# A two-layer diffusion trunk on one core: layer norm's mean held to an upper place, output projection begun with attention's half, adaLN units released by twos

## The chip, the cores and the metric

The kernel runs on one core of one Trainium2 chip. The metric is the device time of one execution in microseconds (us); the time of the kernel before is the median of three runs. Smaller is better.

## The reference

One inference step of a two-layer trunk over T = 384 tokens (128 context tokens, 256 latent tokens), width D = 2048, all in float32. Cut to what this case touches (layer 0, the even one):

```python
sh, sc, gt = split(silu(c) @ w_mod + b_mod, 3)            # adaLN, for each layer
h = rms_norm(x, g) * (1 + sc) + sh
ga, gb, gate_a, q, k, v, gate_b = split(h @ w_in)
a = depthwise_conv(ga * sigmoid(gb), conv_w) + conv_b     # 31 taps
a = silu(layer_norm(a, ln_g, ln_b)) * silu(gate_a)        # 1024 channels: conv's half
b = attention(q, k, v) * silu(gate_b)                     # 8 heads of 128: attention's half
x = x + gt * (concatenate([a, b]) @ w_out)
```

Layer 1 follows with another attention and a short convolution, then a final rms norm.

## The kernel before

Activations lie feature by token: `x["T"]` and `mix` are 16 chunks k of 128 features by 384 tokens. In `mix` of layer 0 chunks 0 to 7 are the conv's half, chunks 8 to 15 attention's half. Every large product is done with float32 operands split in two: `split` makes a high part on ScalarE (ACT) and the rest on VectorE (DVE), `hhi`/`hlo` for the activations and `whi`/`wlo` for a weight tile `raw`, and TensorE (PE) does three products, (hi, hhi), (hi, hlo), (lo, hhi).

A feature pass is `proj_feat`: 256 output features (two PSUM accumulators, a `pair()` out of five banks `acc`), 16 chunks, in two units of 8 chunks, `feat_unit`; a unit is two halves `hf` of four chunks, each with a weight tile of its own. A tile is used by 24 products of 128 x 384, a pass by 96. `whi` and `wlo` have three buffers each (`NHI`, `NLO`), so that a tile's casts wait until PE has left the tile three before it; `raw` has six.

Layer 0 runs feature passes for conv (`w0[0..7]`), then gate_a (`w0[8..11]`), gate_b (`w0[12..15]`), then the output projection `out_proj` (eight passes `fb`, 768 products) and on to layer 1. The conv's 31 taps run on DVE beside the passes, and attention's small products (`s_ps`, `pT_ps`, `o_ps`) stand on PE between the products of the passes. After the first gate_b pass the code calls `ln_mean` (sum of the conv's chunks `lsum`, a product with ones, `mean`) and `ln_center` (subtract, squares, variance `lvar`), after the second the inverse deviation (`rsl` on PE, Newton steps on DVE, `rbl` on PE, copy `rb`) and `ln_out` (a product on DVE and a SiLU on ACT per chunk), and then `mod_rows`, adaLN columns of layer 1 as dot products on DVE (L207, tile `area`). At last L799 multiplies the conv's half into `mix`.

The order on each engine is set by the tile framework, which schedules the whole program by its own timeline and by code order as priority; `tc.add_manual_dep(a, b, NOSYNC)` only forbids it to place a before b, with no semaphore. Each engine then runs its list strictly in that order. All weight loads issue from one queue, SP's, in code order (`sync_load`).

`gemv_q` holds other adaLN columns as units: a load of 1 MB to one of three lent slots (`lent`) and four thin products (`gv`, eight instructions in a trace, as float32 operands that aren't split take two). `pump`, called after each unit of a pass, releases a unit whenever `rate` has added up to one.

Of the kernel before, what the change touches and what calls it, by code (L numbers as in the profile page):

```python
# [17 lines left out]
NOSYNC = mybir.DependencyInfo(mybir.DependencyClass.NoSync, mybir.DependencyReason.DATA)  # L18
# [4 lines left out]
T = 384  # L23
# [28 lines left out]
def trunk(ctx: ExitStack, tc: tile.TileContext, d: dict, o: dict):  # L52
# [39 lines left out]
        if order["hold"] is not None:  # L92
            tc.add_manual_dep(ins, order["hold"].name, SYNC, reason="side loads wait")

    order = {"last": None, "split": None, "hold": None}

    def sync_load(dst, src):
        ins = nc.sync.dma_start(dst, src).ins
# [4 lines left out]
    def load_w(w, k0, nk, f0, nf, raw=None):  # L103
        if raw is None:
            raw = wp.tile([P, nk, nf], F32, tag="raw", name="raw")
        sync_load(raw, w[:, k0:k0 + nk, f0:f0 + nf])
        return raw
# [14 lines left out]
    def gemv_block(w, f0, nf, stat, done):  # L122
        nk = 2048 // nf
        st = {}

        def unit(u):
            if u == 0:
                st["ps"] = ps_gv.tile([P, 512], F32, tag="gv", name="gv")
            ps = st["ps"]
            slot = ring_slot()  # L130
            if slot is not None:
                raws = [load_w(w, nk * u, nk, f0, nf, slot.rearrange("p (k f) -> p k f", f=nf))]
            else:
                raws = [load_w(w, nk * u + nk // 2 * i, nk // 2, f0, nf) for i in range(2)]
            for i in range(nk):
                g = i % 4
                k = nk * u + i
                raw = raws[i * len(raws) // nk]
                nc.tensor.matmul(ps[32 * g:32 * g + 32, :nf], lhsT=stat(k), rhs=raw[:, i % raw.shape[1], :],  # L139
                                 start=(k < 4), stop=(k >= KC - 4))  # L140
            if nk * (u + 1) == KC:
                gs = tmp.tile([P, 512], F32, tag="gs", name="gs", bufs=1)
                nc.scalar.copy(gs[:, :nf], ps[:, :nf])
                done(gs, ps)
        return [lambda u=u: unit(u) for u in range(KC // nk)]

    def mod_tile(layer, part):
        m = const.tile([P, KC, 2], F32, name=f"mod{layer}{part}")
        mods[layer, part] = m
        return m  # L150

    def mod_finish(layer, part, sl, parts):
        n = sl.stop - sl.start
        b = vec(f"mod_b{layer}")[:, 16 * part:16 * part + 16]
        gn = vec(f"norm_g{layer}")
        dst = mods[layer, part][:, sl, :]
        if parts is not None:
            nc.vector.tensor_reduce(dst, parts, AX.X, ALU.add)
        bb = b[:, sl].unsqueeze(2).broadcast_to([P, n, 2])
        nc.vector.tensor_tensor(dst, dst, bb, ALU.add)  # L160
        if part == 1:
            gg = gn[:, sl].unsqueeze(2).broadcast_to([P, n, 2])
            nc.vector.scalar_tensor_tensor(dst, dst, 1.0, gg, ALU.add, ALU.mult)

    def mod_part(layer, part, widths=(512, 512, 512, 512), f0=0):
        if (layer, part) not in mods:
            mod_tile(layer, part)

        def consume(f0, nf, gs, pc):
            n = nf // P  # L170
            for i in range(n):
                nc.tensor.transpose(pc[:, i * P:(i + 1) * P], gs[:, i * P:(i + 1) * P], ident)  # L172
            sl = slice(f0 // P, (f0 + nf) // P)
            mod_finish(layer, part, sl, pc[:, :nf].rearrange("p (k g r) -> p k r g", g=4, r=32)[:, :, 0:2, :])
        units = []
        for nf in widths:
            units += gemv_block(d[f"mod_w{layer}"][4 * part + f0 // 512], f0 % 512, nf, lambda k: cst[:, 2 * k:2 * k + 32],
                                lambda gs, ps, f0=f0, nf=nf: consume(f0, nf, gs, ps))
            f0 += nf
        return units  # L180
# [101 lines left out]
    def split(dst_hi, dst_lo, src):  # L282
        nc.scalar.copy(dst_hi, src)  # L283
        order["split"] = nc.vector.tensor_tensor(dst_lo, src, dst_hi.bitcast(F32), ALU.subtract).ins  # L284
# [28 lines left out]
    gemv_q = []  # L313
    fill_q = []

    bg = {"rate": 0.0, "due": 0.0}

    def pump():
        bg["due"] += bg["rate"]
        while bg["due"] >= 1.0 - 1e-6 and gemv_q:  # L320
            bg["due"] -= 1.0
            gemv_q.pop(0)()

    @contextmanager
    def first():
# [20 lines left out]
    def load_split(w, k0, nk, nf):  # L346
        raw = load_w(w, k0, nk, 0, nf)
        hi = wp.tile([P, nk, nf], F32R, tag="whi", name="whi", bufs=NHI)
        lo = wp.tile([P, nk, nf], F32R, tag="wlo", name="wlo", bufs=NLO)
        split(hi, lo, raw)  # L350
        return hi, lo
# [22 lines left out]
    def feat_unit(pp, w, u, n, begin, end):  # L374
        for hf in range(2):
            hi, lo = load_split(w, 8 * u + 4 * hf, 4, 256)
            for j in range(2):
                fj = slice(j * P, (j + 1) * P)
                for i in range(4):
                    k = 8 * u + 4 * hf + i  # L380
                    for m, (x, y) in enumerate(((hi, hhi), (hi, hlo), (lo, hhi))):
                        ins = nc.tensor.matmul(pp[j][:, :n], lhsT=x[:, i, fj], rhs=y[:, k, :n],  # L382
                                               start=(begin and k % 8 == 0 and m == 0),
                                               stop=(end and k % 8 == 7 and m == 2)).ins
                        order["product"] = ins
            for _ in range(FILL):
                if fill_q:
                    fill_q.pop(0)()
        pump()

    def pair():
        return [acc(f"pf{j}") for j in range(2)]
# [173 lines left out]
            return go  # L566
        return ev

    def out_proj(layer, w, mix, units, each, split_last=0, between=None):
        gate = mods[layer, 2]  # L570
        for k in (*range(8 * units[0], 8 * units[0] + 8), *range(8 * units[1], 8 * units[1] + 8)):
            split(hhi[:, k, :T], hlo[:, k, :T], mix[:, k, :])

        def ev(fb):
            def go(j, ps):
                f = 2 * fb + j
                if layer == 0:
                    s = tmp.tile([P, T], F32, tag="wk", bufs=4, name="go")
                    for g, c0, c1 in GROUPS:
                        nc.scalar.activation(s[:, c0:c1], ps[:, c0:c1], AF.Copy, scale=gate[:, f, g:g + 1])  # L580
                    nc.vector.tensor_tensor(x["T"][:, f, :], x["T"][:, f, :], s, ALU.add)
                else:
                    for g, c0, c1 in GROUPS:
                        nc.vector.scalar_tensor_tensor(x["T"][:, f, c0:c1], ps[:, c0:c1], gate[:, f, g:g + 1],
                                                       x["T"][:, f, c0:c1], ALU.mult, ALU.add)
                each(f)
            return go
        for fb in range(8 - split_last):
            proj_feat(w[fb], ev(fb), units)
        held = {fb: pair() for fb in range(8 - split_last, 8)}  # L590
        for fb, pp in held.items():
            feat_unit(pp, w[fb], units[0], T, True, False)
        if between:
            between()
        for fb, pp in held.items():
            feat_unit(pp, w[fb], units[1], T, False, True)
            for j in range(2):
                ev(fb)(j, pp[j])


    w0 = d["wf0"]
# [18 lines left out]
    for j, nf in enumerate(widths):  # L620
# [7 lines left out]
        last = j == len(widths) - 1  # L628
# [36 lines left out]
    mix = big.tile([P, KC, T], F32, tag="bigB", name="mix0")  # L665
# [47 lines left out]

    def own_slots():
        ring["slots"] = slots
    gates0 = mod_part(0, 2) + mod_part(1, 1, (512,))
    gates0[0] = lambda unit=gates0[0]: (own_slots(), unit())
    gemv_q.extend(bias_q + gates0)
# [32 lines left out]
    def ln_mean():  # L751
        av = tmp.tile([P, T], F32, tag="sacc", name="lsum", bufs=1)
        nc.vector.tensor_tensor(av, apad[:, 0, :T], apad[:, 1, :T], ALU.add)
        for c in range(2, 8):
            nc.vector.tensor_tensor(av, av, apad[:, c, :T], ALU.add)
        pm = aux("mean")
        ins = nc.tensor.matmul(pm[:, :T], lhsT=ones.broadcast_to([P, P]), rhs=av, start=True, stop=True).ins
        tc.add_manual_dep(ins, order["product"].name, NOSYNC, reason="not before its place")
        ln["m"] = tmp.tile([P, T], F32, tag="rb", name="mean", bufs=1)
        nc.scalar.activation(ln["m"], pm[:, :T], AF.Copy, scale=1.0 / CW)  # L760

# [48 lines left out]
    def ahead():  # L810
        drain(gemv_q)
        for k in range(8):
            make_h(1, k)
    out_proj(0, d["w_out0"], mix, (0, 1), each, 2, ahead)


    for k in range(8, KC):
# [6 lines left out]
    mix = big.tile([P, KC, T], F32, tag="bigB", name="mix1")  # L824
# [212 lines left out]
```

## Time and profile before

| | us |
|---|---|
| median of three runs (1300.74 to 1301.24) | 1300.79 |
| the profiled execution | 1300.42 |
| its span, first to last instruction | 1298.6 |
| PE busy in the span | 1257.6 |
| DVE busy | 884.9 |
| ACT busy | 564.6 |
| what lies outside the span (1300.42 less 1298.6) | 1.8 |

Busy times add up what an engine executed. PE is busy for 97% of the span, so that nearly the whole time is its list of products, and what can be had lies in the 41 us in which it stands still and in stretches at a lower granted clock.

### The profile page before, as it was taken

Reading aid. Unit: us, or ns where it says so; the run is one execution under the profiler, and the core shown is the slowest. Engines: PE = TensorE matmul, PEld = TensorE weight load, DVE = VectorE, ACT = ScalarE, POOL = GpSimd, SP = SyncE. Lnnn points to the kernel's source line nnn. Section 1 sums busy time; section 2 is a strip of 40 time slices with the busy share of each in tenths; the row PEclk is TensorE's granted clock in tenths of the full one; section 3 lists DMA queues with packets and bytes.
Section 4 is the critical chain, followed back from the end, with each engine's and each line's share of the span. In section 5 each row is a group of like instructions: output and inputs, shape, how many; then the busy total and the mean of one; then the engine's idle time right before and its main releaser. Section 6 shows DMA issues by size and latency. Waiting matters only on the chain.

```text
span 1298.6 us, 17795 instructions
## 1 busy us (share of the span) xinstructions
PE 1257.6 (97%) x6856; PEld 1116.1 (86%) x6856; DVE 884.9 (68%) x1507; ACT 564.6 (43%) x989; POOL 96.3 (7%) x137
## 2 busy tenths in 40 slices
PE   6999999999999999599999999999999999999997
PEld 3566676888978799499999988899999999999997
DVE  2244688998989975999976942354443599994443
ACT  3345432664465655433464632254444423343322
POOL 0211100000000000111100000000000011101110
PEclk9999999999999999799999999999999999999999
DMA  9989987787554344387743444333333578844422
GB/s 367 401 305 356 342 318 289 301 321 250 188 201 146 116 163 154 108 266 255 251 155 119 129 130 125 120 120 115 100 97 106 166 259 271 267 148 129 130 65 97
DMA packets 67620, 257.97 MB, mean 199 GB/s; under 512 B 7056, under 2 KB 11408, under 8 KB 59984
## 3 DMA queue, kind: packets, MB, share of 16 engines
q1 hardware_dynamic: 54736, 203.51, 45.4%
q0 software_dynamic: 12656, 53.23, 12.0%
q8 instruction: 53, 0.87, 0.3%
q14 instruction: 31, 0.25, 0.1%
q10 hardware_dynamic: 144, 0.10, 0.0%
HBM read 253.15 MB, written 3.67 MB: 198 GB/s over the span
## 4 chain that ended last, share of the span: by engine, by line
PE 96%; DVE 2%; DMA 1%; ACT 0%; issue 0%; SPq 0%; DVEq 0%; ACTq 0%
PE pf L382 68%; PE pt L361 10%; PE q L612 6%; PE gv L139 5%; PE s_ps L505 2%; PE o_ps L530 2%; PE pT_ps L526 1%; DMA ring<-in_mod_w 1%; PE y_ps L921 1%; PE gv L172 0%; PE qT_ps L491 0%; PE gv L676 0%; DVE mix L799 0%; DVE apad L773 0%; DVE area L207 0%
## 5 line engine op out<-in xcount | busy, mean ns | idle before, releaser
L382 PE MATMUL pf<-hhi,whi 128*128 128x384 f32 (+1 forms) x1664 | 568.9, 342 | 10.9 <-ACT hhi L283 10.6
L382 PE MATMUL pf<-hlo,whi 128*128 128x384 f32 (+1 forms) x1664 | 570.9, 343 | 5.0 <-DVE hlo L284 5.0
L382 PE MATMUL pf<-hhi,wlo 128*128 128x384 f32 (+1 forms) x1664 | 565.7, 342 | 1.2 <-DVE wlo L284 1.2
L284 DVE TENSOR_TENSOR wlo<-raw,whi 128x1024 fp32r<-128x1024 f32 x256 | 313.0, 1224 | 285.5 <-ACT whi L283 280.6
L283 ACT CAST whi<-raw 128x1024 fp32r<-128x1024 f32 x256 | 268.3, 1050 | 475.1 <-PE pf L382 267.4
L382 PEld LDWEIGHTS pf<-hhi,whi 128*128 128x128 f32 x1664 | 313.6, 189 | 31.9 <-issue 14.6
L382 PEld LDWEIGHTS pf<-hhi,wlo 128*128 128x128 f32 x1664 | 313.7, 189 | 12.2 <-issue 4.7
L382 PEld LDWEIGHTS pf<-hlo,whi 128*128 128x128 f32 x1664 | 314.1, 189 | 10.8 <-DVE hlo L284 5.5
L207 DVE CUSTOM_DVE_ANT_0 area<-area,crow 128x1024 f32<-128x1024 f32 x128 | 151.3, 1218 | 4.9 <-PE o_ps L530 4.4
L702 DVE SCALAR_TENSOR_TENSOR cv<-apad,cw,cv 128x399 f32<-128x399 f32 x240 | 138.7, 628 | 0.0
L361 PE MATMUL pt<-wlo,hhi 128*128 128x512 f32 x192 | 75.8, 395 | 0.0
L361 PE MATMUL pt<-whi,hhi 128*128 128x512 f32 x192 | 75.4, 396 | 0.0
L361 PE MATMUL pt<-whi,hlo 128*128 128x512 f32 x192 | 74.1, 395 | 0.0
L91 POOL DMA_DIRECT2D area<-in_modT x64 | 33.9, 531 | 457.6 <-DVE sm L207 223.8
L276 POOL TENSOR_TENSOR sacc<-sacc,sqf 128x384 f32<-128x384 f32 x28 | 33.5, 1196 | 176.4 <-ACT sqf L275 175.6
L361 PEld LDWEIGHTS pt<-whi,hhi 128*128 128x128 f32 x192 | 36.0, 188 | 11.0 <-ACT hhi L308 1.7
L612 PE MATMUL q<-whi,hhi 128*128 128x512 f32 x96 | 41.1, 428 | 4.4 <-ACT hhi L295 4.4
L361 PEld LDWEIGHTS pt<-whi,hlo 128*128 128x128 f32 x192 | 35.9, 188 | 10.0 <-DVE wlo L284 1.7
L139 PE MATMUL gv<-ring,cst 128*32 128x512 f32 (+1 forms) x288 | 35.6, 582 | 8.6 <-DMA ring<-in_mod_w 7.7
L361 PEld LDWEIGHTS pt<-wlo,hhi 128*128 128x128 f32 x192 | 36.1, 188 | 9.1 <-issue 0.8
L513 ACT ACTIVATE pr<-s_ps,nm 128x384 f32<-128x384 f32 (+1 forms) x48 | 24.4, 509 | 44.2 <-DVE nm L512 34.4
L612 PE MATMUL q<-wlo,hhi 128*128 128x512 f32 x96 | 40.5, 422 | 0.0
(186 smaller groups left out, 1005.9 us busy)
## 6 DMA issues: line engine op xcount, KB each, us to landing
raw<-in_wf SPq DMA_DIRECT2D x144, 512.0 KB, 4.5
ring<-in_mod_w SPq DMA_DIRECT2D x32, 1024.0 KB, 7.0
raw<-in_w_out SPq DMA_DIRECT2D x64, 512.0 KB, 4.1
area<-in_modT POOLq DMA_DIRECT2D x64, 512.0 KB, 5.2
lent<-in_mod_w SPq DMA_DIRECT2D x20, 1024.0 KB, 4.9
raw<-in_wq SPq DMA_DIRECT2D x32, 512.0 KB, 8.7
raw<-in_wt SPq DMA_DIRECT2D x24, 512.0 KB, 3.6
lent<-in_modT POOLq DMA_DIRECT2D x8, 1024.0 KB, 8.2
```

The costliest lines, as they stand in the source:

```text
L91: ins = nc.gpsimd.dma_start(dst, src).ins
L139: nc.tensor.matmul(ps[32 * g:32 * g + 32, :nf], lhsT=stat(k), rhs=raw[:, i % raw.shape[1], :], start=(k < 4), stop=(k >= KC - 4))
L207: ins = nc.vector.tensor_tensor_reduce(out=raw if g else junk, in0=raw, in1=crow[:, g, h * n:(h + 1) * n], scale=1.0, scalar=0.0, op0=ALU. ...
L276: eng.tensor_tensor(av, av, s, ALU.add)
L283: nc.scalar.copy(dst_hi, src)
L284: order["split"] = nc.vector.tensor_tensor(dst_lo, src, dst_hi.bitcast(F32), ALU.subtract).ins
L361: nc.tensor.matmul(pp[t], lhsT=x[:, k, tt], rhs=y[:, i, :], start=(k == 0 and n == 0), stop=(k == KC - 1 and n == 2))
L382: ins = nc.tensor.matmul(pp[j][:, :n], lhsT=x[:, i, fj], rhs=y[:, k, :n], start=(begin and k % 8 == 0 and m == 0), stop=(end and k % 8 == ...
L505: nc.tensor.matmul(ps, lhsT=mix[:, h0 + h, t * P:(t + 1) * P], rhs=kT[:, kv, c0:c0 + nk * P], start=True, stop=True)
L530: nc.tensor.matmul(po, lhsT=v[:, slots[j], kv * HD:(kv + 1) * HD], rhs=pT[:, j, :], start=(j == 0), stop=(j == nk - 1))
L612: nc.tensor.matmul(pq[b][t], lhsT=x[:, k, tt], rhs=y[:, 0, 512 * b:512 * b + 512], start=(k == 0 and n == 0), stop=(k == KC - 1 and n == 2))
L702: nc.vector.scalar_tensor_tensor(st["o"], apad[:, c, j:j + CVW], cw[:, c, j:j + 1], st["o"], ALU.mult, ALU.add)
```

## The change

Three edits. First, the scheduler may not place the first product of the fifth weight half after `ln_mean` (that is the first product of the third gate_b pass) before the product `mean`. Second, layer 0's output projection takes chunks 8 to 15 first, then 0 to 7, and its first two passes run by halves: both passes' attention units, then both passes' conv units, with four accumulators held. The last two passes ran by halves before, and keep their order (chunks 0 to 7 first). Third, once the lent slots belong to the adaLN units, `pump` releases two at a time.

```diff
+    bg = {"rate": 0.0, "due": 0.0, "set": 1}
     def pump():
         bg["due"] += bg["rate"]
-        while bg["due"] >= 1.0 - 1e-6 and gemv_q:
-            bg["due"] -= 1.0
-            gemv_q.pop(0)()
+        while bg["due"] >= bg["set"] - 1e-6 and gemv_q:
+            bg["due"] -= bg["set"]
+            for _ in range(bg["set"]):
+                if gemv_q:
+                    gemv_q.pop(0)()
...
             hi, lo = load_split(w, 8 * u + 4 * hf, 4, 256)
+            order["halves"] += 1
...
+                        if order["must"] and order["must"][1] == order["halves"]:
+                            tc.add_manual_dep(ins, order["must"][0].name, NOSYNC, reason="not behind this place")
+                            order["must"] = None
                         order["product"] = ins
...
+        def by_halves(fbs, units, between=None):
+            held = {fb: pair() for fb in fbs}
+            for fb, pp in held.items():
+                feat_unit(pp, w[fb], units[0], T, True, False)
+            if between:
+                between()
+            for fb, pp in held.items():
+                feat_unit(pp, w[fb], units[1], T, False, True)
+                for j in range(2):
+                    ev(fb)(j, pp[j])
+        by_halves(range(split_first), units)
+        for fb in range(split_first, 8 - split_last):
             proj_feat(w[fb], ev(fb), units)
...
+        by_halves(range(8 - split_last, 8), units[::-1], between)
...
     def own_slots():
         ring["slots"] = slots
+        bg["set"] = 2
...
+        order["must"] = (ins, order["halves"] + 5)
...
-    out_proj(0, d["w_out0"], mix, (0, 1), each, 2, ahead)
+    out_proj(0, d["w_out0"], mix, (1, 0), each, 2, 2, ahead)
```

No instruction is added or taken away but for the order; the number of products, loads and casts is the same. Three places show what the scheduler made of it (line numbers of the kernel before stand some lines lower in the changed one).

On PE, at the third gate_b pass (accumulators pf_4146 and pf_4147; pf_3858 is the second pass's). Before, the last of the last head group's products (`o_ps`) and the mean stand behind 60 of the third pass's 96 products:

```order
L382 MATMUL pf_4146<-hlo,whi 128x384
L382 MATMUL pf_4146<-hhi,wlo 128x384
L530 MATMUL o_ps<-pT,kv 128x512
L757 MATMUL mean<-lsum,ones 128x384
L382 MATMUL pf_4147<-hhi,whi 128x384
```

Now:

```order
L385 MATMUL pf_3858<-hhi,wlo 128x384
L532 MATMUL pT_ps<-ident,pr 128x128 x12
L536 MATMUL o_ps<-pT,kv 128x512 x3
L768 MATMUL mean<-lsum,ones 128x384
L385 MATMUL pf_4146<-hhi,whi 128x384
L385 MATMUL pf_4146<-hlo,whi 128x384
```

The mean stands ahead of the third pass, and the last head group's transposes and products stand right before it in one block, with no product of a pass among them. Behind it, `rsl` follows after 85 products instead of 89, and `rbl` after 123 of the 192, where it stood behind all 132 that were left.

On DVE, from the fourth gate_b pass's end into the output projection (`rb` is the inverse deviation, `sg` a SiLU of gate_b, `area` the dot products of `mod_rows`). Before:

```order
L284 TENSOR_TENSOR wlo<-raw,whi 128x1024
L565 TENSOR_TENSOR mix_1217<-mix_1217,sg 128x384 x3
L773 TENSOR_TENSOR apad<-apad,rb 128x384 x8
L565 TENSOR_TENSOR mix_1217<-mix_1217,sg 128x384
L207 ISA area,sm_4046<-area,crow 128x1024
L207 ISA sm_4046 128x1
L284 TENSOR_TENSOR hlo<-mix_1217,hhi 128x384 x3
L799 TENSOR_TENSOR mix_1217<-mix_1217,apad 128x384 x7
```

Now:

```order
L785 TENSOR_TENSOR apad<-apad,rb 128x384 x8
L207 ISA area,sm_4046<-area,crow 128x1024
L207 ISA sm_4046 128x1
L811 TENSOR_TENSOR mix_1217<-mix_1217,apad 128x384 x4
L284 TENSOR_TENSOR wlo<-raw,whi 128x1024
L811 TENSOR_TENSOR mix_1217<-mix_1217,apad 128x384
L207 ISA area,sm_4046<-area,crow 128x1024
L207 ISA sm_4046 128x1
L207 ISA area,sm_4046<-area,crow 128x1024
L207 ISA sm_4046 128x1
L811 TENSOR_TENSOR mix_1217<-mix_1217,apad 128x384 x3
L284 TENSOR_TENSOR hlo<-mix_1217,hhi 128x384 x5
```

Before, `hlo` of chunks 8 to 11 stood well ahead of these rows, and the x3 are chunks 12 to 14. Now no `hlo` stands ahead of the last L811; the x5 are, by their operands, chunks 8, 9, 0, 10, 1, and what follows is: wlo, hlo of 11, 2, 3, two L207, the SiLU's product for chunk 14, hlo of 12, 13, 4, wlo, the product for chunk 15, hlo of 5, 6, 7, wlo, two L207, hlo of 14, 15.

On SP's queue, where the adaLN units' loads begin (`lent` is 1 MB, `raw` one weight tile of 512 KB). Before:

```order
L98 DMA lent<-in_mod_w 128x2048 x2
L98 DMA raw<-in_wf 128x1024 x2
L98 DMA lent<-in_mod_w 128x2048
L98 DMA raw<-in_wf 128x1024 x2
L98 DMA lent<-in_mod_w 128x2048 x2
```

Now:

```order
L98 DMA lent<-in_mod_w 128x2048
L98 DMA raw<-in_wf 128x1024 x2
L98 DMA lent<-in_mod_w 128x2048 x2
L98 DMA raw<-in_wf 128x1024 x2
L98 DMA lent<-in_mod_w 128x2048 x2
L98 DMA raw<-in_wf 128x1024 x4
```

The loads come in pairs, with four to six weight tiles between two pairs.

## Rows read from the trace of the kernel before

**Rows 1.** PE's waits, whole run: waiter, releaser, us in total, times, longest.
```profile
PE pf L382 <- ACT hhi L283: 10.6, 1, 10.6
PE pf L382 <- DVE hlo L284: 5.0, 1, 5.0
```
**Rows 2.** Stretches: busy us of each engine (instructions), PE's granted clock, DMA share, GB/s.
```profile
core 0: us, PE busy (x) PEld busy (x) DVE busy (x) ACT busy (x) POOL busy (x), PEclk, DMA share, GB/s
...
500.00:540.00 40.00, 24.42 (x136) 23.55 (x135) 34.24 (x73) 24.41 (x44) 2.84 (x2) 0.81 0.39 128
540.00:610.00 70.00, 70.00 (x396) 70.00 (x396) 67.81 (x111) 25.36 (x40) 10.20 (x19) 0.99 0.74 243
...
680.00:745.00 65.00, 65.00 (x371) 64.78 (x370) 50.36 (x107) 37.64 (x82) 1.44 (x2) 1.00 0.39 121
```
**Rows 3.** PE in order of time: start, us, instruction, idle before and its releaser.
```profile
521.10 0.93 PE L256 MATMUL rbl<-diag,ones 128*128 128x128 f32 x6
532.65 1.01 PE L382 MATMUL pf<-hhi,whi 128*128 128x384 f32 x2 [10.62 <-ACT hhi L283]
538.61 0.69 PE L382 MATMUL pf<-hlo,whi 128*128 128x384 f32 x1 [4.96 <-DVE hlo L284]
...
541.88 0.34 PE L382 MATMUL pf<-hhi,wlo 128*128 128x384 f32 x1
```
**Rows 4.** The chain that ended last, 480 to 560 us: start, us, what.
```profile
490.98 0.44 PE pT_ps L526 x4
...
495.94 0.86 PE o_ps L530 x2
496.80 0.65 PE mean L757 x2
497.44 15.60 PE pf L382 x89
513.04 0.56 PE rsl L240 x6
```
**Rows 5.** ACT in order of time, 470 to 545 us.
```profile
486.89 1.08 ACT L527 COPY pT<-pT_ps 128x512 f32<-128x512 f32 x2 [2.69 <-PE pT_ps L526]
...
521.11 1.04 ACT L283 CAST whi<-raw 128x1024 fp32r<-128x1024 f32 x1 [2.66 <-PE pf L382]
...
525.32 4.89 ACT L774 ACTIVATE apad<-apad,vecs 128x384 f32<-128x384 f32 x8
```
**Rows 6.** DVE in order of time, 522 to 545 us.
```profile
522.18 1.23 DVE L284 TENSOR_TENSOR wlo<-raw,whi 128x1024 fp32r<-128x1024 f32 x1 [0.75 <-ACT whi L283]
...
524.73 3.83 DVE L773 TENSOR_TENSOR apad<-apad,rb 128x384 f32<-128x384 f32 x8
...
528.95 1.22 DVE L207 CUSTOM_DVE_ANT_0 area<-area,crow 128x1024 f32<-128x1024 f32 x1
...
530.09 1.49 DVE L284 TENSOR_TENSOR hlo<-mix,hhi 128x384 fp32r<-128x384 f32 x3
531.50 3.36 DVE L799 TENSOR_TENSOR mix<-mix,apad 128x384 f32<-128x384 f32 x7
```
**Rows 7.** AdaLN units on PE, in the chain of the whole run.
```profile
239.96 1.85 PE gv L139 x16
...
246.02 1.00 PE gv L139 x8
```
**Rows 8.** ACT at 250 us: a weight tile's cast that waited for its load.
```profile
250.55 1.05 ACT L283 CAST whi<-raw 128x1024 fp32r<-128x1024 f32 x1 [5.35 <-DMA raw<-in_wf]
```
**Rows 9.** PE at 45 us, after 2.20 us idle (0.76 us idle stood just before).
```profile
45.87 0.50 PE L612 MATMUL q<-whi,hhi 128*128 128x512 f32 x1 [2.20 <-ACT hhi L295]
...
47.38 0.63 PE L612 MATMUL q<-wlo,hhi 128*128 128x512 f32 x1
```
**Rows 10.** Stretches of 1 us, columns as in rows 2: the clock after two idle times.
```profile
47.00:48.00 1.00, 1.00 (x4) 0.81 (x3) 1.00 (x4) 1.00 (x4) 0.00 (x0) 0.50 1.00 416
...
50.00:51.00 1.00, 1.00 (x5) 0.84 (x4) 0.00 (x0) 0.00 (x0) 0.00 (x0) 0.89 1.01 416
...
524.00:525.00 1.00, 0.00 (x0) 0.00 (x0) 1.00 (x3) 1.00 (x4) 0.00 (x0) 0.84 0.54 70
525.00:526.00 1.00, 0.00 (x0) 0.00 (x0) 1.00 (x3) 1.00 (x3) 0.00 (x0) 0.50 0.89 336
...
541.00:542.00 1.00, 1.00 (x5) 1.00 (x5) 1.00 (x2) 0.00 (x0) 0.00 (x0) 0.62 0.00 0
```

More of the change, by code (lines that the diff above doesn't have):

```diff
@@ L93, in side_load @@
             tc.add_manual_dep(ins, order["hold"].name, SYNC, reason="side loads wait")
-    order = {"last": None, "split": None, "hold": None}
+    order = {"last": None, "split": None, "hold": None, "must": None, "halves": 0}
     def sync_load(dst, src):
@@ L314, in trunk @@
     fill_q = []
-    bg = {"rate": 0.0, "due": 0.0}
+    bg = {"rate": 0.0, "due": 0.0, "set": 1}
     def pump():
         bg["due"] += bg["rate"]
-        while bg["due"] >= 1.0 - 1e-6 and gemv_q:
-            bg["due"] -= 1.0
-            gemv_q.pop(0)()
+        while bg["due"] >= bg["set"] - 1e-6 and gemv_q:
[3 more added lines that the diff above has]
+                    gemv_q.pop(0)()
     @contextmanager
@@ L567, in gate_mul, with out_proj @@
         return ev
-    def out_proj(layer, w, mix, units, each, split_last=0, between=None):
+    def out_proj(layer, w, mix, units, each, split_first=0, split_last=0, between=None):
         gate = mods[layer, 2]
@@ L587, in ev @@
             return go
-        for fb in range(8 - split_last):
-            proj_feat(w[fb], ev(fb), units)
[L590 to L598, printed above, removed]
+        def by_halves(fbs, units, between=None):
[10 more added lines that the diff above has]
+        for fb in range(split_first, 8 - split_last):
+            proj_feat(w[fb], ev(fb), units)
+        by_halves(range(8 - split_last, 8), units[::-1], between)
     w0 = d["wf0"]
```

## The prediction

> **What bounds the kernel now.** I read PE's waits first [rows 1]. Of the 41 us that PE stands still, 15.6 us are two waits, each met once: 10.6 us for a high part made by ACT and 5.0 us for a low part made by DVE. The table of stretches says where: from 500 to 540 us PE is busy for 24.42 of 40 us, and both before and after the engine is full [rows 2]. PE's own list gives the place [rows 3]. The last product of layer norm, `rbl`, ends at 522.03; the next product, the output projection's first, starts at 532.65, the third at 538.61. In between DVE and ACT work through the inverse deviation's eight products, eight SiLUs, eight products into `mix` and the splits [rows 5, 6], and nothing else is ready for PE, since the projection begins with the conv's half.
>
> The stall costs more than its length, because the granted clock fell. It goes from full (2.4 GHz) to half (1.2 GHz) within the microsecond 524 to 525, 2 to 3 us after PE had stopped, and comes back between 541 and 542, after PE had worked again for 3 us [rows 10]. At full clock a product of 128 x 384 follows the one before by 15.60 / 89 = 0.1753 us [rows 4]. From 522.03 to 541.88 PE did 12 products, 2.10 us of work, so this place costs 19.85 - 2.10 = **17.75 us**. That is all the change can win here.
>
> **Held mean.** Before, the mean ends at 497.45 [rows 4], with 132 gate products still to come, and `rbl` stands behind all of them. Now 192 products follow the mean and `rbl` stands behind 123. The work up to the end of the gate passes is unchanged, so if nothing waits that end stays at 522.0, and `rbl` comes 69 x 0.1753 = 12.1 us before it.
>
> What the hold costs is at the block. Twelve transposes (0.44 per four), six `o_ps` (0.43 each) and the mean (0.65) are 1.32 + 2.58 + 0.65 = 4.55 us on PE [rows 4]. Before, products of a pass lay between them and hid the copies on ACT; now nothing does. The transposes have two PSUM banks for three groups, ACT needs 0.54 us per copy [rows 5], and in the new order a weight tile's cast (1.04) stands ahead of the three copies, which can only start when PE has left the second pass. So ACT's first copy ends 1.04 + 0.2 + 0.54 = 1.8 us after that (the 0.2 is an estimate for the hand-overs between engines; a single one, from the cast's end at 522.15 to `wlo`'s start at 522.18, took 0.03 [rows 5, 6]). PE has done eight transposes by 0.88, waits 0.9, does the last four, and goes on when the second copy is done, 0.1 later. **Cost 1.0 us.** The bounds: nothing, if ACT is early; and at the other end the 60 products that stood between pass start and mean, 10.5 us, if all the cover is needed.
>
> **Output projection begun with attention's half.** The end of the gate passes becomes 522.0 + 1.0 - 0.5 (below) = 522.5. Counted back from it, `rbl` ends at 522.5 - 12.1 = 510.4. DVE's products with `rb` then start about 0.8 later (one ACT operation of 4.89 / 8 = 0.61 and hand-overs), at 511.2. From here I add up DVE's list in the new order, with the durations of rows 6 taken start to start: 3.83 for the eight products, 1.15 for a dot product (L207), 0.48 for a product into `mix`, 1.14 for a weight tile, 0.47 for a split.
>
> - To the first `hlo` that PE needs, chunk 8: 3.83 + 1.15 + 8 x 0.48 + 1.14 + 2 x 1.15 + 0.47 = 12.7, at 523.9. PE can only do two products (0.35) after 522.5 and waits 1.05.
> - To `hlo` of chunk 12: four splits, a tile, three splits, two dot products, a product, a split, 1.88 + 1.14 + 1.41 + 2.30 + 0.47 + 0.47 = 7.7, at 531.6. PE has 28 products that need only chunks 8 to 11 (two passes' tiles are mixed here), 4.9 us, and is through at 528.8. It waits 2.8.
> - To chunk 15: 0.94 + 1.14 + 0.47 + 1.41 + 1.14 + 2.30 + 0.94 = 8.3, at 539.9. PE has 58 products before it, 10.2 us, until 541.8, and doesn't wait.
> - The first tile of the conv's half must wait for a buffer: PE leaves the tile three before it late, because passes are mixed. A cast and a low part then stand in the way, of whose 1.04 + 1.14 some eight products cover a part. I take 0.75.
>
> The new waits add up to **4.6 us**, against 17.75. The bounds are 0 (if DVE comes to the splits before PE needs them) and 9.2, twice the sum, since a DVE list that is full has no room to recover.
>
> By the same addition the conv's half itself is ready by 536 and PE wants it at about 543: it is hidden by 96 products of attention's half, 16.8 us. Four dot products are moved behind, 4 x 1.15 = 4.6 us of DVE work that comes later. DVE is full to 610 (67.81 of 70), but from 680 to 745 it is idle for 14.6 us [rows 2], and the last columns are wanted only when layer 1 has begun. I take 0; without that cover it would cost up to 4.6.
>
> **Units by twos.** Eight instructions of one unit take 1.00, sixteen of two units 1.85 [rows 7], so a joined pair saves 0.15. In the new order 20 units stand in 14 groups instead of 17, and fewer are cut by other products: a gain of 0.5 us, with bounds 0 and 1. The loads of a pair need two slots before the weight tiles behind them on SP's queue can issue. The tightest place is the first pair, whose second load waits for a unit 48 products (8.4 us) before its weight tile is used. In the trace of before such a tile was waited for at 250.55 [rows 8] and still came before PE needed it. I take 0; the other bound is 4 us there.
>
> **The sum**: 17.75 - 1.0 - 4.6 + 0.5 = 12.6 us. On the profiled execution's own 1300.42 (span 1298.6 and 1.8 around it) this gives 1287.8; it lies 0.37 under the median of the runs, so I forecast **1288.2**. One per five hundred, 2.6 us, is about what a measurement of this kernel can tell from no change.
>
> **A rule against it.** At 45 us PE stood idle for 0.76 and 2.20 us with 0.66 us of work between, and a microsecond after it had resumed the clock was at half, and full again only about 50 us [rows 9, 10]. My second gap, 2.8 us, is about as long as the time at 522 after which the clock fell. The Trainium skill (TensorE: Matmul & The Clock Gate, section "HAM oscillation — how this bites in real kernels") warns that a kernel which idles between bursts of products pays the slow start after each pause again; by that rule several short waits may be no better than one. What a fall would cost, from rows 3: ten products at half clock took 541.88 - 538.61 = 3.27 us instead of 1.75, so 1.5 us, once or twice.
>
> **The rivals.**
> 1. *The forecast*, gaps as summed, clock full: 1286.5 to 1289.5. Chance 0.50.
> 2. *The clock falls in the new gaps, or DVE's list is later than summed.* For it: the length of the second gap; DVE is at 34.24 of 40 us in this stretch [rows 2], and its operations don't get fewer. Against it: both new gaps have full bursts of products between them. One fall and half again the gaps, 1.5 + 2.3: **1292**. Chance 0.25 (0.15 of it the clock's rule).
> 3. *Everything is hidden*: DVE reaches chunk 12 in time and the block's copies are early. 17.75 + 0.5 less 1.5: **1284**. Against it: no `hlo` of attention's half stands ahead of the last L811. Chance 0.10.
> 4. *Pairs starve the weight tiles*: the first tile behind the pair is late by 4 us [rows 8]: **1292**. Chance 0.08.
> 5. *Slower, by the held mean.* PE can do no product of the third pass before the mean, so each microsecond by which the last head group's softmax or the sum of the conv's chunks is late is idle time on PE, with no cover. It takes over the gain at 12.6 us of extra wait, and shows as slower from 15.2. In the order of before the mean began 60 products and 3.90 us of transposes and `o_ps` after the third pass's start, 14.4 us, and no row shows how much sooner its inputs could have come, so a wait of 10 us is thinkable (then 1298 to 1300, the clock's fall included); a slower result needs the taps of the conv to be late too. Chance 0.04 slower, 0.03 for no change to be told.
>
> The range, from the third to the dearer end of the second and fourth: 1284 to 1293. Faster by over 0.2%: 0.93, within 0.2%: 0.03, slower: 0.04.
>
> **What would show it.** In the profile after: `rbl` some 12 us before the first projection product, that product at about 520 to 523, two waits of PE on `hlo` of 1 and 3 us where 15.6 us were, the third gate_b pass starting about 1 us late behind the mean, and the granted clock of the stretch at or near full. The start of the third projection pass, which in the trace of before is at 541.88 + 180 x 0.1753 = 573.4 (180 of the first two passes' 192 products stand behind 541.88), should be near 573.4 - 12.6 = 560.8. I am wrong if PE waits before the mean for more than 2 us, if `hlo` waits exceed 8 us, or if PE waits on weight tiles between 230 and 480 us.

## The result and the profile after

The changed kernel takes 1285.95 us (1285.85 to 1286.07, four runs) against 1301.01 (1300.74 to 1301.28): 15.06 us less, ratio 0.9884 with an interval of 0.9867 to 0.9901. The forecast was 1288.2 in a range of 1284 to 1293. The likeliest case's own range (1286.5 to 1289.5) is missed by half a microsecond, and behind the near hit stand two large terms that the sum didn't hold.

PE's waits after, in the form of [rows 1]: waiter, releaser, us in total, times, longest.

```profile
PE pf L385 <- DVE hlo L284: 3.6, 2, 2.5
...
PE pf L385 <- ACT whi L283: 1.9, 2, 1.6
...
PE pT_ps L532 <- ACT pT L533: 0.6, 1, 0.6
```

The two waits of [rows 1], 10.6 and 5.0, are now two waits of 1.1 and 2.5 on `hlo`. New are 1.6 us for a weight tile and 0.6 us in the block at the mean. PE's list gives the places.

```profile
476.28 0.34 PE L385 MATMUL pf<-hhi,wlo 128*128 128x384 f32 x1
476.45 1.04 PE L532 MATMUL pT_ps<-ident,pr 128*128 128x128 f32 x8
478.06 0.65 PE L532 MATMUL pT_ps<-ident,pr 128*128 128x128 f32 x4 [0.57 <-ACT pT L533]
...
482.05 0.34 PE L385 MATMUL pf<-hlo,whi 128*128 128x384 f32 x1
...
504.13 0.83 PE L256 MATMUL rbl<-diag,ones 128*128 128x128 f32 x6
504.71 0.42 PE L385 MATMUL pf<-hhi,whi 128*128 128x384 f32 x1
504.98 0.34 PE L385 MATMUL pf<-hlo,whi 128*128 128x384 f32 x1
...
516.90 0.51 PE L385 MATMUL pf<-hhi,whi 128*128 128x384 f32 x2
518.53 0.45 PE L385 MATMUL pf<-hlo,whi 128*128 128x384 f32 x1 [1.12 <-DVE hlo L284]
...
523.17 0.51 PE L385 MATMUL pf<-hhi,whi 128*128 128x384 f32 x2
526.18 0.44 PE L385 MATMUL pf<-hlo,whi 128*128 128x384 f32 x1 [2.50 <-DVE hlo L284]
526.45 0.34 PE L385 MATMUL pf<-hhi,wlo 128*128 128x384 f32 x1
...
554.70 0.34 PE L385 MATMUL pf<-hhi,whi 128*128 128x384 f32 x1
...
664.63 0.83 PE L240 MATMUL rs<-ones,sacc 128*128 128x1 f32 x6 [0.19 <-DVE sacc L276]
667.04 0.45 PE L385 MATMUL pf<-hhi,whi 128*128 128x386 f32 x1 [1.58 <-ACT whi L283]
...
668.15 1.01 PE L385 MATMUL pf<-hhi,whi 128*128 128x386 f32 x2
...
671.21 0.39 PE L385 MATMUL pf<-hhi,whi 128*128 128x386 f32 x1
...
729.13 0.39 PE L363 MATMUL pt<-whi,hhi 128*128 128x512 f32 x1
```

The same places in the trace before: the third gate_b pass's first product, and the start of layer 1.

```profile
482.21 0.34 PE L382 MATMUL pf<-hhi,whi 128*128 128x384 f32 x1
...
682.98 0.72 PE L240 MATMUL rs<-ones,sacc 128*128 128x1 f32 x6
...
743.85 0.39 PE L361 MATMUL pt<-whi,hhi 128*128 128x512 f32 x1
```

A gap costs a little more than its idle time, since the first product after it is late as well: from 516.90 to 518.82, and from 523.17 to 526.45, where three products take 0.53 us, 1.39 and 2.75 us are lost. The stretches (columns as in [rows 2]) tell the granted clock: full through the projection's start, half at 668 us, a microsecond after the wait that follows `rs` of layer 1's norm.

```profile
500.00:540.00 40.00, 36.39 (x209) 35.72 (x208) 37.55 (x66) 22.17 (x38) 5.10 (x5) 1.00 0.46 136
...
666.00:667.00 1.00, 0.00 (x0) 0.00 (x0) 0.00 (x0) 1.00 (x3) 0.64 (x1) 1.00 0.00 0
668.00:669.00 1.00, 0.87 (x4) 0.85 (x4) 1.00 (x3) 1.00 (x4) 0.00 (x0) 0.50 0.00 0
```

From these rows the account of the gain on PE, against the trace before:

| place | forecast | measured | from |
|---|---|---|---|
| up to the end of the second gate_b pass (units by twos) | +0.5 | +5.8 | end of that pass at 482.21 before, at 476.45 after |
| block at the mean | -1.0 | -0.87 | from 476.45 to the third pass's second product at 482.05, less 4.55 of work and 0.18 for its first product |
| stall at the projection | +17.75 - 4.6 | +17.75 - 4.14 | the two gaps; the conv's first tile was not waited for |
| start of layer 1 | 0 | -3.63 | first `rs` to first `pt`: 60.87 before (682.98 to 743.85), 64.50 after (664.63 to 729.13) |
| sum | 12.6 | 14.9 | from the last norm's `rs` (1283.31, 1268.60): 14.7 |

From the first `pt` to that last `rs` both traces take the same time (539.46 and 539.47), so nothing else of the program moved. (Medians differ by 15.06, the two profiled executions by 14.35: that of before, 1300.42, lies 0.59 under its median.)

### The profile page after: what moved, and what is told of

Same layout as the page of the kernel before. It is cut to its first block, busy times and chain, and to the rows that moved or that the text cites. A ratio compares the mean times of both kernels' runs of the same rounds, so it can differ in the third digit from the quotient of the medians.

```text
span 1284.3 us, 17787 instructions
## 1 busy us (share of the span) xinstructions
PE 1252.4 (98%) x6856; PEld 1115.6 (87%) x6856; DVE 885.0 (69%) x1507; ACT 561.2 (44%) x987; POOL 96.1 (7%) x137
## 4 chain that ended last, share of the span: by engine, by line
PE 95%; DVE 2%; ACT 1%; issue 1%; DMA 1%; SPq 0%; DVEq 0%; ACTq 0%
PE pf L385 67%; PE pt L363 11%; PE q L622 6%; PE gv L139 5%; PE s_ps L511 2%; PE o_ps L536 2%; PE pT_ps L532 1%; DMA ring<-in_mod_w 1%; PE y_ps L933 1%; PE gv L172 0%; PE qT_ps L497 0%; DVE wlo L284 0%; ACT whi L283 0%; DVE hlo L284 0%; PE gv L686 0%
## 5 line engine op out<-in xcount | busy, mean ns | idle before, releaser
L207 DVE CUSTOM_DVE_ANT_0 area<-area,crow 128x1024 f32<-128x1024 f32 x128 | 151.6, 1220 | 6.5 <-PE o_ps L536 4.4
```

Of the source, the lines that this page charges most:

```text
L207: ins = nc.vector.tensor_tensor_reduce(out=raw if g else junk, in0=raw, in1=crow[:, g, h * n:(h + 1) * n], scale=1.0, scalar=0.0, op0=ALU. ...
```

## The experiments

**All eight combinations.** Each edit was put back by its lines:

```diff
-        bg["set"] = 2
...
-        order["must"] = (ins, order["halves"] + 5)
...
-        by_halves(range(8 - split_last, 8), units[::-1], between)
+        by_halves(range(8 - split_last, 8), units, between)
...
-    out_proj(0, d["w_out0"], mix, (1, 0), each, 2, 2, ahead)
+    out_proj(0, d["w_out0"], mix, (0, 1), each, 0, 2, ahead)
```

Expected of the held mean alone (only_mean), the projection alone (only_out), the twos alone (only_twos), and the first two together (mean_out):

> The kernel before with the held mean alone (output projection still begun with the conv's half, units released one at a time). Theory O (overlap: the held mean and the changed projection remove the same stall, each nearly all of it by itself): rbl comes 12 us before the gate passes end, so the conv's half is nearly ready when the projection wants it; of 17.75 us stay a block cost of 0.85 and a wait of about 1.4, and the time is near 1285.5, or near 1289 if the late weight cast at the start of layer 1 (3.6 us in the changed kernel) comes too. Theory B (both edits are needed, gains add): the conv's half is still wanted first and late, the stall shrinks by some 6 us only, time near 1295.

> The kernel before with the output projection begun with attention's half alone. Theory O: the low parts of chunks 8 to 11 are made during the last gate pass as in the kernel before, 96 products of attention's half (16.8 us) cover the work from rbl to the conv's low parts (about 17 us), a wait of 1 to 2 us remains, no block cost: time near 1285. Theory B: the conv's half is 12 us later than in the changed kernel and PE waits for it by some 10 us: near 1294.

> The kernel before with the units released by twos alone. Theory S (the four products of a unit write four strips of 32 rows and run beside each other, so that a piece of one, two or three products takes as long as four; the new order has 22 such rounds in 16 pieces where 26 in 23 stood): 4 x 0.86 + 7 x 0.14 = 4.4 us less, near 1296.5. The prediction's term (a joined pair saves 0.15, three pairs fewer): 0.5 less, near 1300.5. Theory P (pairs starve weight tiles): slower, near 1305.

> The changed kernel without the release by twos. Theory O: the two edits together leave more than either alone, since DVE's list makes all low parts behind the conv's products: block 0.85, waits 1.4 and 2.75 as in the changed kernel, 17.75 - 5.0 = 12.8 us less than before and near 1288.3 without the late cast at the start of layer 1, near 1291 with it; slower than only_mean and only_out. Theory B: faster than both of these. Theory S wants it 4.4 us above the changed kernel's 1285.95, near 1290.4; the prediction's term 0.5 above it.

Expected of the kernels that lack one edit each, without the projection (mean_twos) and without the held mean (out_twos):

> The changed kernel with the output projection as before (conv's half first). Theory O: the held mean alone already removes most of the stall, and the release by twos adds its own 6 us (measured on PE up to the mean in the first runs): 1292.9 - 6 = near 1287, within 2 us of the changed kernel. Theory B (the changed projection is needed for the gain): 1292 or more.

> The changed kernel without the held mean. Theory O: the changed projection alone removes the stall but for about 3.5 us (wait and half clock), and the twos add 6 us: 1291.7 - 6 = 1285.7 with the waits at the start of layer 1 that the projection alone showed (4.7 us), down to 1281 without them: the held mean is worth nothing beside the changed projection, or costs. Theory B: 1290 or more.

Measured (medians of four or five runs; the gain is against the kernel before on the same chip, "lost" is PE's time beyond products at full clock, from its list in one execution, at the projection's start and at the start of layer 1; for the held mean alone that execution is the fastest of five, 1290.61 us in a spread to 1293.91):

| held mean | projection | twos | us | ratio, interval | gain | lost at the projection | lost at layer 1 |
|---|---|---|---|---|---|---|---|
| - | - | - | | | 0 | 17.8 | 0 |
| x | - | - | 1292.91 | 0.9936 (0.9924 to 0.9948) | 7.9 | 6.8 | 0 |
| - | x | - | 1291.69 | 0.9930 (0.9918 to 0.9943) | 9.1 | 3.9 | 4.9 |
| - | - | x | 1293.26 | 0.9943 (0.9931 to 0.9956) | 7.5 | 17.4 | 0 |
| x | x | - | 1289.70 | 0.9915 (0.9902 to 0.9929) | 11.1 | 5.7 | 0.6 |
| x | - | x | 1287.47 | 0.9899 (0.9885 to 0.9912) | 13.2 | 9.3 | 0 |
| - | x | x | 1280.36 | 0.9842 (0.9829 to 0.9856) | 20.3 | 0.6 | 3.1 |
| x | x | x | 1285.95 | 0.9884 (0.9867 to 0.9901) | 15.1 | 4.1 | 3.6 |

(With the twos alone the loss at the projection is two waits, 9.4 and 4.5 us, and some twenty products at half clock.) Theory O's main point holds: the held mean and the projection remove the same stall. Alone they win 7.9 and 9.1, together 11.1 without the twos, where added gains (theory B) would be 17.0. Its times and its order do not hold. For either edit alone it was 7 us too good, further off than theory B (1295 and 1294), since it counted neither a fall of the clock (both kernels show one) nor, in only_out, the waits at layer 1, and took the waits on `hlo` too short. It had mean_out slower than only_mean and only_out; mean_out is the faster, as theory B said (every run of it, 1289.23 to 1290.15, lies under every run of the other two). In mean_out the two waits were those of the changed kernel, and the clock fell behind the second.

Beside the projection and the twos the held mean costs 5.2 to 5.6 us. Beside the projection without the twos it wins 2.0: at the projection it loses there too (5.7 against 3.9), but the loss at layer 1 is 0.6 instead of 4.9.

Theory P is out. The twos alone bring 7.5, more than theory S's 4.4, and far from the prediction's 0.5. Beside the held mean they bring 5.3, beside the projection 11.2, beside both 4.0. What they save on PE ahead of the block at the mean is 5.8 in the trace after; most of the rest is what the new order loses or saves in the last two columns.

**Units cut in two.** On the kernel before:

```diff
+            if bg["cut"] and nk * (u + 1) < KC:
+                products(range(2))
+                bg["rest"].append(lambda: products(range(2, nk)))
+            else:
+                products(range(nk))
```

> The kernel before, with fifteen of the twenty units cut in two on purpose: two of the four products are issued at once, the other two behind the next 24 products of a pass. Nothing is left out. In this order the thin products take 35 rounds (a round is what one to four products into different strips take) where the kernel before has 26. Theory S (a piece of two takes as long as four): 9 x (0.86 + 0.14) = 9 us more, near 1310. The prediction's term (a start of 0.15 per piece, the products themselves by their number): 9 x 0.15 = 1.3 more, near 1302.

Measured: 1309.76 us against 1300.65, 9.1 more (ratio 1.0074, 1.0062 to 1.0087); theory S said 9. The groups of thin products by line (busy us, mean ns), first before:

```profile
L139 PE MATMUL gv<-lent,cst 128*32 128x512 f32 x160 | 26.9, 603 | 0.0
```

then after:

```profile
L139 PE MATMUL gv<-lent,cst 128*32 128x512 f32 x160 | 22.1, 601 | 0.0
```

and in the cut kernel:

```profile
L140 PE MATMUL gv<-lent,cst 128*32 128x512 f32 x160 | 36.3, 603 | 0.0
```

The same 160 instructions of the same mean length occupy PE for 26.9, 22.1 and 36.3 us: the fewer cuts, the more of them run beside each other. Before, two pieces of a unit that was cut by other products stand in PE's list like this:

```profile
298.23 1.04 PE L139 MATMUL gv<-lent,cst 128*32 128x512 f32 x2
299.21 0.66 PE L491 MATMUL qT_ps<-ident,nat 128*128 128x128 f32 x4
...
300.02 1.06 PE L139 MATMUL gv<-lent,cst 128*32 128x512 f32 x6
301.01 0.44 PE L382 MATMUL pf<-hhi,whi 128*128 128x384 f32 x1
301.28 0.34 PE L382 MATMUL pf<-hlo,whi 128*128 128x384 f32 x1
```

A quarter of the unit takes 0.98, the other three quarters 0.99, and [rows 7] show 1.00 for a whole one. Six of the twenty units were cut so before, two after.

**One cast behind the last column.** On the changed kernel, and on the one without the held mean:

```diff
+        if order["casts"]:
+            order["casts"] -= 1
+            if not order["casts"]:
+                tc.add_manual_dep(ins, order["go"].name, NOSYNC, reason="column first")
...
+    order["casts"] = 4
     conv_pair(0, True)
```

ACT after, in order of time, where layer 0's projection ends:

```profile
660.10 1.05 ACT L283 CAST whi<-raw 128x1024 fp32r<-128x1024 f32 x1 [1.49 <-issue]
...
661.48 0.71 ACT L586 ACTIVATE go<-pf,mod 128x128 f32<-128x128 f32 x2
663.46 0.53 ACT L275 ACTIVATE sqf<-xT 128x384 f32<-128x384 f32 x1 [1.26 <-DVE xT L587]
663.89 2.17 ACT L290 ACTIVATE h<-xT,mod 128x128 f32<-128x128 f32 x6
665.96 1.03 ACT L283 CAST whi<-raw 128x1024 fp32r<-128x1024 f32 x1
```

The last column's product with the gate, `go`, had its accumulator complete at 656.8 and started at 661.48, behind a cast that began at 660.10. All that follows is that late, the tile that PE waits for at 667.04 too.

> The changed kernel, with one weight tile's cast at the end of layer 0's projection forbidden ahead of the last column's product with the gate on ACT. Theory J (in the changed kernel this cast waits for PE to leave a buffer, the last column, the last squares and the chunks 8 to 11 of layer 1 wait behind it, and PE is idle and then at half clock: 3.6 us): near 1282.4. Rival (PE would wait there for the reciprocal root anyway): near 1286.

> The changed kernel without the held mean, and with one weight tile's cast forbidden ahead of the last column at the end of layer 0's projection, as in the run junction. In out_twos the waits at the start of layer 1 add up to about 3.3 us of PE's time (restarts counted in). Theory J: up to 2 us of them go, near 1278.5. Rival (there DVE's dot products, which end at 670 us, set the end): no change, 1280.4.

Measured on the changed kernel 1283.41 us (0.9867, 0.9854 to 0.9881), 2.5 less than the change. The intervals of the two overlap, so it is the trace that decides: from `rs` to `pt` PE takes 61.66 instead of 64.50, while in this run the clock fell at the projection's second gap and took 1.5 back. Theory J holds there. On the kernel without the held mean it fails: no gain, but 1282.55 (0.9863, 0.9848 to 0.9878), 2.2 above out_twos, about as much as the intervals can separate. PE's waits there:

```profile
PE pf L389 <- ACT hhi L283: 1.9, 1, 1.9
PE pf L389 <- ACT whi L283: 1.6, 3, 1.0
```

The 1.9 us on `hhi` of layer 1 are new, and the clock fell behind them. So the hold isn't a cure but one more order, and the loss at layer 1 (0 to 4.9 us over the kernels) depends on how the scheduler happens to interleave casts, columns and chunks.

**Attention's low parts first.** On the changed kernel:

```diff
         for c in range(8):
-            nc.vector.tensor_tensor(mix[:, c, :], mix[:, c, :], apad[:, c, :T], ALU.mult)
+            ins = nc.vector.tensor_tensor(mix[:, c, :], mix[:, c, :], apad[:, c, :T], ALU.mult).ins
+            tc.add_manual_dep(ins, lows[3].name, NOSYNC, reason="low parts first")
```

with `lows` the low parts' instructions on DVE in `out_proj`'s order (8 to 15, then 0 to 7), and the conv's products emitted behind the splits of attention's half. For dots_behind `mod_rows` is called there too, and its dot products may not stand before the low part of chunk 15:

```diff
-            shifts.append(mod_rows(1, 0, 3, vring, ln["out"]))
-            scales = [mod_rows(1, 1, j, vring, ln["out"]) for j in (1, 2, 3)]
...
+        shifts.append(mod_rows(1, 0, 3, vring, order["split"]))
+        scales.extend(mod_rows(1, 1, j, vring, order["split"]) for j in (1, 2, 3))
```

> The changed kernel, with DVE's eight products of the conv's half into mix forbidden ahead of the low part of chunk 11. Theory L (the two waits on hlo come only from the place of attention's low parts behind the conv's products, not from missing inputs): the first wait (1.4 us with its restart) goes, the second (2.75 us) shrinks to about 1, since chunk 12's low part comes some 1.8 us earlier: near 1283. Rival (the high parts or the last SiLUs are late themselves): both waits stay, near 1286.

> As low_parts_first, and the dot products of the adaLN columns are also held behind the last low part. Theory L: both waits go (4.1 us), and the dot products come some 7 us later. If they are still early enough for layer 1: near 1282. If not (they end at 656 us in the changed kernel, layer 1 reads the last of them at 669): what was won is lost at the start of layer 1, 1285 or more.

DVE after, up to the two low parts that PE waits for:

```profile
505.85 3.83 DVE L785 TENSOR_TENSOR apad<-apad,rb 128x384 f32<-128x384 f32 x8
...
516.51 1.50 DVE L811 TENSOR_TENSOR mix<-mix,apad 128x384 f32<-128x384 f32 x3
517.92 2.43 DVE L284 TENSOR_TENSOR hlo<-mix,hhi 128x384 fp32r<-128x384 f32 x5
...
522.80 1.22 DVE L207 CUSTOM_DVE_ANT_0 area<-area,crow 128x1024 f32<-128x1024 f32 x1
...
523.95 1.23 DVE L207 CUSTOM_DVE_ANT_0 area<-area,crow 128x1024 f32<-128x1024 f32 x1
...
525.09 0.56 DVE L571 TENSOR_TENSOR mix<-mix,sg 128x384 f32<-128x384 f32 x1
525.56 1.50 DVE L284 TENSOR_TENSOR hlo<-mix,hhi 128x384 fp32r<-128x384 f32 x3
```

and in dots_behind:

```profile
512.87 1.50 DVE L284 TENSOR_TENSOR hlo<-mix,hhi 128x384 fp32r<-128x384 f32 x3 [1.58 <-ACT hhi L283]
...
515.79 0.55 DVE L284 TENSOR_TENSOR hlo<-mix,hhi 128x384 fp32r<-128x384 f32 x1
516.26 2.43 DVE L823 TENSOR_TENSOR mix<-mix,apad 128x384 f32<-128x384 f32 x5
...
520.48 1.02 DVE L284 TENSOR_TENSOR hlo<-mix,hhi 128x384 fp32r<-128x384 f32 x2
```

Measured: low_parts_first 1284.73 (0.9879, 0.9863 to 0.9896), only 1.2 less than the change, which the intervals don't separate. In its trace the first wait is gone, the second is still 1.99 (theory L had about 1), and a `wlo` comes 0.80 late. dots_behind 1279.80 (0.9841, 0.9826 to 0.9855), 6.2 less than the change: PE waits for no `hlo` any more, and the dot products, 667 us at the last instead of 656, are early enough. What is lost at layer 1 is 1.9 instead of 3.6, which theory L had not forecast; with the 4.1 of the two waits this makes the gain. So the order of DVE's list made both waits: all low parts came in time once those of chunks 8 to 11 stood ahead of the conv's products, and all eight ahead of the dot products.

**The same without the held mean.** The kernel of dots_behind with one line taken out:

```diff
-        order["must"] = (ins, order["halves"] + 5)
```

> The kernel of dots_behind without the held mean. Theory L (once DVE's list puts attention's low parts first, both orders of the mean leave no stall at the projection, and the held mean only costs its block, 0.8 us with the restart): 1279.0, within 1 us of dots_behind. Rival (the held mean gives DVE the time to make the conv's half, and without it PE waits for it): 1282 or more.

Measured 1280.94 (0.9857, 0.9840 to 0.9874; single runs 1279.9 to 1285.2), the profiled run 1279.90 against 1279.91 of dots_behind. PE waits for no `hlo` here either. The two can't be told apart, so theory L's claim that the held mean then costs 0.8 us stays open; the rival is out.

All three, dots_behind, out_twos and dots_no_mean, beat the kernel before by far more than is uncertain. dots_behind and out_twos also beat the changed kernel (their intervals lie wholly under its own); that of dots_no_mean, up to 0.9874, reaches a little into it (0.9867 to 0.9901). Among themselves the three aren't separated.

## Why the prediction was right, and where its sum was not

- *What bounds the kernel: right.* The 17.75 us at the projection shrank to 4.1. "That is all the change can win here" held for the place, but the change won 5.8 elsewhere.
- *Held mean: the cost is right, the worth was never asked.* The block's cost, 0.87 (1.0 forecast), came by the rows named: ACT's tile cast, two copies, and PE's wait of 0.57.

```profile
476.47 1.04 ACT L283 CAST whi<-raw 128x1024 fp32r<-128x1024 f32 x1 [1.06 <-PE pf L385]
477.43 1.08 ACT L533 COPY pT<-pT_ps 128x512 f32<-128x512 f32 x2
```

`rbl` ends at 504.96, 11.9 us before the projection's first product (12.1 were forecast). But the sum credited the whole stall to the edits together and never asked what each does alone. The eight combinations show that beside the changed projection the early `rbl` costs time at the projection (1.8 us without the twos, 3.5 with them), and with the twos it is a loss in all: it puts layer norm's products on DVE in front of attention's low parts, which the projection now wants first. Without it these low parts stand ahead, as in out_twos (lost at the projection: 0.6 us), where the first of them comes 8.7 us before layer norm's products:

```profile
510.64 0.56 DVE L284 TENSOR_TENSOR hlo<-mix,hhi 128x384 fp32r<-128x384 f32 x1 [0.23 <-ACT hhi L283]
...
519.37 3.83 DVE L784 TENSOR_TENSOR apad<-apad,rb 128x384 f32<-128x384 f32 x8
```

- *Output projection: right in place and size.* Waits of 1.12 and 2.50 (with restart 1.39 and 2.75) against 1.05 and 2.8 forecast, by adding up DVE's list in the new order. The third term, 0.75 for a buffer, did not come.
- *Units by twos: the term that was mis-sized, 0.5 against 5.8.* The step that failed: "Eight instructions of one unit take 1.00, sixteen of two units 1.85 [rows 7], so a joined pair saves 0.15." It took a piece's time to go with its number of products. In fact four products into four strips of 32 rows run beside each other, so that a cut unit pays twice: four cuts fewer, 3.4 us, and seven pieces fewer (16 instead of 23 in the traces, where the prediction counted 14 groups instead of 17), 1.0, make 4.4. Added up in the traces, from each piece's first product to the start of what follows it, the pieces take 25.3 us before and 21.0 after, 4.3 less. The remaining 1.5 us lie outside them: the first product behind a piece costs PE about 0.1 more than another (301.01 to 301.28 where 0.175 is usual), and seven pieces fewer make 0.7 of it; the rest is open. The Trainium skill (TensorEngine Tiling (Array Packing), section "Tiling Modes") says that different tiles can execute in parallel and that a change of mode drains the engine. The rows agree with the first, and the forecast should have drawn on it; the second no run here shows, since the same 0.1 stands behind `rbl`, which uses the whole array (504.71 to 504.98).
- *"I take 0" for the columns moved behind: the loss came, but by another way.* At the start of layer 1 3.6 us were lost, with ACT's list (a cast ahead of the last column) and not DVE's dot products as the main cause: in the run junction 2.8 of them are gone. The prediction asked there for the columns alone and put no price on any other change of order.
- *The clock, rival 2's rule.* It did not fall in the two gaps forecast, but did at layer 1, a microsecond after 1.58 us of idle time. That ten products at half clock cost about 1.5 was right (here nine, from 668.15 to 671.21, took 3.06 instead of 1.58).
- *Rivals 3 to 5.* Not everything was hidden; no pair starved a weight tile; PE did not wait for the mean. The other rows named: the projection's first product comes at 516.90, ahead of the 520 to 523 named as a sign, and the third projection pass starts at 554.70 (162 of 192 products behind the second gap), where 560.8 was forecast; of the 6.1 between these 5.3 are the units'.

That the forecast came so near was in part luck: two terms that it didn't hold, +5.3 and -3.6, partly cancelled.

## What to carry to other kernels

Price each edit alone and beside the others: two that aim at the same stall don't add, and one may undo the order on which the other rests, or change an order far behind both. When an engine's list is full, ask which of its results the waiting engine wants first, and put those first; here, with the other two edits in place, that was worth more than starting the whole chain earlier. The products that share the array by strips here are counted in rounds, and a round that is cut in two is paid twice.

## What the runs showed of the hardware

The clock does not follow the length of one gap alone. In mean_out the same two waits stand as after the change, 1.11 and 2.50 us, with the same restart at full clock, and 1.2 us later the clock fell:

```profile
532.00:533.00 1.00, 0.71 (x4) 0.71 (x5) 1.00 (x3) 0.32 (x1) 0.00 (x0) 1.00 0.74 229
533.00:534.00 1.00, 1.00 (x6) 0.99 (x5) 1.00 (x2) 0.00 (x0) 0.00 (x0) 0.71 0.66 246
534.00:535.00 1.00, 1.00 (x5) 1.00 (x4) 1.00 (x3) 0.19 (x1) 0.00 (x0) 0.50 0.01 4
```

After the change it stayed full at that place. In the other kernels it fell behind a wait of 1.95 us in only_out and 2.05 in only_mean, and stayed full behind 1.99 in low_parts_first. What sets these apart is not found in the profiles, and the cause is open. A fall cost about 1.5 us in each of these three (ten or eleven products at 0.32 us instead of 0.175).
